# Layer 0's operator products and scan steps on VectorE, its squares on ScalarE and TensorE, and a last norm that takes token blocks one by one

## The chip, the cores and the metric

The kernel is one program on one core of a Trainium2 chip. The core's engines are TensorE (PE: matmuls; PEld: its weight loads), VectorE (DVE), ScalarE (ACT), GpSimd (POOL) and SyncE (SP), which issues most DMAs. Each engine takes its instructions in the order in which they stand in its own queue; an instruction whose inputs aren't ready holds up all behind it. The metric is the time of one execution on the device in microseconds. The kernel before takes 2677.52 us, the median of three runs (2677.16 to 2686.56).

## The reference

One step of a streaming encoder with two layers and width 1024, on 1024 prompt tokens and 8 running streams of 16 tokens (1152 columns in all). Layer 0 mixes an S5 state space model with a gated DeltaNet; layer 1 is sliding-window attention; each is followed by a SwiGLU. Cut to what the change touches:

```python
def rmsnorm(x, w):
    xf = x.astype(jnp.float32)
    y = xf * lax.rsqrt(jnp.mean(xf * xf, axis=-1, keepdims=True) + RMS_EPS)
    return (y * w.astype(jnp.float32)).astype(x.dtype)

def l2norm(x):
    return x * lax.rsqrt(jnp.sum(x * x, axis=-1, keepdims=True) + L2_EPS)

# S5, in chunks of 64 tokens
lam_bar = jnp.exp(lam * dt)
b_bar = ((lam_bar - 1.0) / lam)[..., None] * lax.complex(b_re, b_im)
def step(carry, u_blk):
    bu = jnp.einsum('gpc,btgc->btgp', b_bar, u_blk.astype(jnp.complex64))
    bu = bu.at[:, 0].add(lam_bar * carry)
    _, xs = lax.associative_scan(combine, (a_blk, bu), axis=1)
    y_blk = jnp.einsum('gcp,btgp->btgc', c, xs).real
    return xs[:, -1], y_blk

# DeltaNet: causal conv of width 4 and silu on q, k, v; q and k through l2norm;
# 4 heads of 128 in chunks of 64 with a triangular solve, then a recurrence over chunks
```

## The kernel before, in words

Activations lie with features on partitions: x is four tiles of 128 partitions by 2 feature chunks by 1152 tokens, so there are 8 chunks of features (k) and 3 blocks of 384 tokens (b). An fp32 product is made of three matmuls of split operands (whi, wlo, as in L320 to L322 and L459 to L461); the feed-forward products use a scheme with fewer products, whose panels B11, T1, B21, B22, T2, T3, T4 are summed into x by L836 and L888 as they come out of the banks.

Layer 0 runs in this order. Norm 0 (the loop over b from L987): ScalarE squares the 8 chunks of a block, POOL adds them in pairs (L1000), and `rms` (L366 and on) sums the four pairs over partitions by fp32 matmuls with a matrix of ones (L376). Meanwhile `s5_coefs` builds the S5 operators: a chain of small POOL and ScalarE steps makes lambda's powers (c tiles, L1676 to L1754), then for each of four parts m VectorE and POOL multiply the powers by B and C (L1777 to L1800, `every` at L1750). Their results lb and cl go out by DMA and come back as matmul operands, first for the states XE (pe, L1084). TensorE meanwhile projects the input; its bank evictions ut (L976) and zz (L1042) are VectorE's.

Then comes the scan over chunks: 15 dependent steps, each with two multiplications by the powers L (L1099) and two adds (L1100, L1101), all on POOL; 8 small steps that carry the state FE between groups of 16 chunks (L1105 to L1107), and 7 times two products of 128x512 on POOL (L1111), added to XE by VectorE (L1112, L1113). Beside it run the four DeltaNet heads: projections come out of banks into cr (L1134 to L1137, VectorE), the convolution is four VectorE steps (L1144, L1146), silu makes cy (ScalarE and VectorE, L1152, L1169), the squares of q and k are POOL's (L1164), summed by matmuls (L333), and the head's products A and AQ are finished by VectorE (L1201 to L1209). After the last head come a triangular solve, transfers and the recurrence, then the output product and layer 0's feed-forward.

The scheduler of the framework orders each engine's queue from its own model of times and from priorities that the code gives (`Sooner`). So the order is a result of the whole program, and it changes when an instruction changes its engine.

The last norm is a closure `final` (L1628 to L1648) that the last feed-forward calls through `fill` as chunks of x get final. It squares and adds chunks as they come (`square_in`), calls `rms` for a block, and then scales: chunks 0, 3 and 6 by ScalarE and POOL (L1641, L1642), the other five by VectorE (L1644); an output DMA takes two chunks (L1646). In the code, `final` is set up when panel T2 is done, for all three blocks (L897 and on).

## Time and profile before

| | |
|---|---|
| median of 3 runs | 2677.52 us |
| the profiled execution | 2678.2 us |
| its span in the trace | 2676.4 us |
| TensorE (PE) busy | 2524.3 us, 94% |
| VectorE (DVE) busy | 1986.1 us, 74% |
| POOL busy | 1624.0 us, 61% |
| ScalarE (ACT) busy | 1187.3 us, 44% |

The time of the profiled execution includes 1.8 us around the span. A share over the whole span is a mean over stretches that are bounded by different engines; the stretches that the change touches are the first 430 us and the last 30, and the rows below are taken from these. A busy time of an engine in the trace is from an instruction's start to its end, whatever held it up inside.

### The profile page before, as it was taken

What the parts mean: (1) busy time and instruction counts of PE and PEld (TensorE: products, weight loads), DVE (VectorE), ACT (ScalarE), POOL (GpSimd) and SP (SyncE); (2) the same over time, 40 slices, a digit from 0 to 9 for tenths busy, and PEclk for the clock granted to TensorE, in tenths of its full rate; (3) what the DMA queues carried; (4) which work ended last, traced back from release to release, by engine and by line L of the source; (5) the groups of instructions that cost most, each with busy time, mean ns of one, the idle gap of its engine ahead of it and who ended that gap; (6) DMA issues with size and microseconds to landing.
All of it is one profiled execution on the core that took longest, in us unless ns stands there. A gap on an engine that the chain in (4) does not pass through costs nothing.

```text
span 2676.4 us, 40734 instructions
## 1 busy us (share of the span) xinstructions
PE 2524.3 (94%) x14897; PEld 2403.3 (90%) x14897; DVE 1986.1 (74%) x3255; ACT 1187.3 (44%) x2411; POOL 1624.0 (61%) x1659
## 2 busy tenths in 40 slices
PE   7898899999899999989999999999899999989996
PEld 5787798998799999989998988788789999989996
DVE  7847874567877877788867245667878777788967
ACT  5234466344634444444334145655644444444333
POOL 8739532125598888878633012214598888878735
PEclk9899999999999999989999999999999999989998
DMA  6432377643132222244212200203122222243211
GB/s 211 122 121 72 109 230 225 190 130 118 37 106 76 75 76 87 84 158 134 84 50 103 74 25 25 96 31 103 40 96 89 75 77 75 86 167 127 90 50 71
DMA packets 164167, 267.23 MB, mean 100 GB/s; under 512 B 34188, under 2 KB 123948, under 8 KB 162928
## 3 DMA queue, kind: packets, MB, share of 16 engines
q1 hardware_dynamic: 163392, 262.28, 30.4%
q8 instruction: 117, 1.92, 0.3%
q10 hardware_dynamic: 576, 2.36, 0.2%
q14 instruction: 82, 0.67, 0.1%
HBM read 186.92 MB, written 79.51 MB: 100 GB/s over the span
## 4 chain that ended last, share of the span: by engine, by line
PE 69%; POOL 11%; DVE 10%; DMA 4%; issue 4%; ACT 2%; SPq 0%; DVEq 0%; POOLq 0%; ACTq 0%
PE pa L461 7%; PE pa L459 7%; PE pa L460 7%; PE pd L459 4%; PE pd L460 4%; PE pd L461 4%; PE pg L320 3%; PE b L459 3%; PE pg L322 3%; PE pg L321 3%; PE b L460 3%; PE b L461 3%; PE pg L1549 2%; PE pg L1550 2%; PE pg L1551 2%
## 5 line engine op out<-in xcount | busy, mean ns | idle before, releaser
L459 PE MATMUL pa<-u,whi 128*128 128x384 f32 x904 | 307.2, 341 | 20.0 <-ACT whi L541 10.3
L460 PE MATMUL pa<-u,whi 128*128 128x384 f32 x904 | 306.1, 339 | 1.1 <-DVE u L269 1.1
L461 PE MATMUL pa<-u,wlo 128*128 128x384 f32 x904 | 298.8, 339 | 7.7 <-DVE wlo L542 7.7
L541 ACT CAST whi<-x 128x1024 fp32r<-128x1024 f32 (+2 forms) x184 | 132.2, 745 | 256.9 <-PE pa L460 164.6
L460 PE MATMUL pd<-g,whi 128*128 128x384 f32 x708 | 241.2, 341 | 0.0
L459 PE MATMUL pd<-g,whi 128*128 128x384 f32 x708 | 240.1, 339 | 0.0
L461 PE MATMUL pd<-g,wlo 128*128 128x384 f32 x708 | 238.2, 338 | 0.0
L542 DVE TENSOR_TENSOR wlo<-x,whi 128x1024 fp32r<-128x1024 f32 (+2 forms) x184 | 210.4, 1165 | 24.4 <-ACT whi L541 24.3
L1907 POOL TENSOR_SCALAR p<-p,rd 128x192 f32<-128x192 f32 (+3 forms) x80 | 59.1, 741 | 249.6 <-DVE rd L1901 132.9
L459 PEld LDWEIGHTS pa<-u,whi 128*128 128x128 f32 x904 | 171.5, 190 | 24.9 <-ACT whi L541 13.9
L297 ACT CAST whi<-raw 128x1024 fp32r<-128x1024 f32 x113 | 116.8, 1048 | 172.5 <-PE pg L321 76.0
L537 POOL TENSOR_TENSOR x<-x 128x256 f32<-128x256 f32 (+1 forms) x186 | 171.2, 942 | 25.5 <-DVE wlo L542 18.7
L298 DVE TENSOR_TENSOR wlo<-raw,whi 128x1024 fp32r<-128x1024 f32 x113 | 164.7, 1460 | 21.6 <-ACT whi L297 20.4
L537 POOL TENSOR_TENSOR x<-raw 128x256 f32<-128x256 f32 (+1 forms) x186 | 169.2, 931 | 18.9 <-DVE wlo L542 11.0
L461 PEld LDWEIGHTS pa<-u,wlo 128*128 128x128 f32 x904 | 171.5, 190 | 9.2 <-DVE wlo L542 9.0
L537 POOL TENSOR_TENSOR cm<-raw 128x256 f32<-128x256 f32 (+1 forms) x150 | 145.1, 990 | 47.3 <-DVE wlo L542 18.9
L460 PEld LDWEIGHTS pa<-u,whi 128*128 128x128 f32 x904 | 171.7, 190 | 2.1 <-DVE u L269 1.7
L459 PE MATMUL pa<-u,x 128*128 128x384 f32 x428 | 146.6, 343 | 5.3 <-ACT x L541 2.8
L320 PE MATMUL pg<-h0h,whi 128*128 128x384 f32 x384 | 136.1, 354 | 12.3 <-DVE ut L976 11.4
L460 PE MATMUL pa<-u,x 128*128 128x384 f32 x428 | 145.6, 340 | 0.0
L461 PE MATMUL pa<-u,x 128*128 128x384 f32 x428 | 142.4, 341 | 0.0
L796 DVE TENSOR_TENSOR g<-gf,g 128x384 fp32r<-128x384 f32 x132 | 136.4, 1060 | 5.4 <-ACT g L795 5.4
(744 smaller groups left out, 8223.5 us busy)
## 6 DMA issues: line engine op xcount, KB each, us to landing
gf<-d_g SPq DMA_DIRECT2D x44, 576.0 KB
raw<-in_wd_dram SPq DMA_DIRECT2D x44, 512.0 KB
raw<-in_wg_dram SPq DMA_DIRECT2D x24, 512.0 KB
raw<-in_wu_dram SPq DMA_DIRECT2D x24, 512.0 KB
raw<-in_win_dram SPq DMA_DIRECT2D x21, 512.0 KB
x<-in_wg_dram SPq DMA_DIRECT2D x20, 512.0 KB
x<-in_wu_dram SPq DMA_DIRECT2D x20, 512.0 KB
d_r<-x SPq DMA_DIRECT2D x24, 384.0 KB
```

Of the source, the lines that this page charges most:

```text
L297: S.copy(hi, raw)
L298: V.tensor_sub(lo, raw, hi)
L320: PE.matmul(p[:, :BW], hi[:, c], rh, start=(i == 0), stop=False)
L321: PE.matmul(p[:, :BW], hi[:, c], rl, start=False, stop=False)
L322: PE.matmul(p[:, :BW], lo[:, c], rh, start=False, stop=(i == len(ks) - 1))
L459: PE.matmul(p, hi[:, c], uh, start=start, stop=False, skip_group_check=more)
L460: PE.matmul(p, hi[:, c], ul, start=False, stop=False, skip_group_check=more)
L461: PE.matmul(p, lo[:, c], uh, start=False, stop=stop, skip_group_check=more)
L537: (P.tensor_add if sg > 0 else P.tensor_sub)(cm[:, 256 * j:256 * (j + n)], fa, ga)
L541: S.copy(hi[:, c], src)
L542: V.tensor_sub(lo[:, c], src, hi[:, c])
L796: eng.tensor_sub(op[1], t, op[0])
```

## The change

Four parts lie in layer 0's mixer. In norm 0 POOL's twelve adds are gone and the matmuls with ones sum all 8 squares of a block (24 in place of 12). In `s5_coefs` the products t2, t3, tl and tc (16 instructions) are VectorE's. In the scan, all of POOL's 60 step instructions, the 24 small ones and the 14 of 128x512 are VectorE's. The 24 squares of `l2norms` are ScalarE activations. The fifth part replaces `final` by a class `Final`: block 0 is squared, normed and sent out as soon as its panels are final, before the last panels of the other blocks; the partition sums take more parts by matmul (2, 3 and 6 for the three blocks, where it was 3 each); the scale is left in the PSUM bank p and read from there by the products (L1696 of the new file); ScalarE and POOL take chunks 0 to 2 of block 0 and 0 and 1 of block 1, and none of block 2; the table of logarithms is loaded once, at block 0.

```diff
--- before.py
+++ after.py
@@ -890,12 +890,26 @@
                                 fill(x, 4 + m, 1, 4 + m)
                             if n == "B22":
                                 fill(x, m, 2, 4 + m)
+                                if m == 3 and not nxt:
+                                    fin.out(x, 1)
+                                    fin.out(x, 2)
                     if q < 2 and e == 0:
                         for m in range(4):
                             into([(W[i], 512 * i2, G[i][f"f{i2}"]) for i in range(2) for i2 in range(2)] + plain(4 * q + m, 0), m, x[:, 4 * q + m, blk(0)])
+                    if last and not nxt and q == 1 and e == 0:
+
+                        t = [hp.tile([128, 4, BW], F32, name="sq", tag="h", bufs=4 * NB) for _ in range(4)]
+                        fin = Final([a[:, i] for a in t for i in range(4)])
+                        fill = fin.fill
+                        for k in range(KC):
+                            fill(x, k, 0, k)
+                        fin.out(x, 0)
+                        for k in range(4):
+                            fill(x, k, 1, k)
                     if last and n == "T2":
                         for m in range(4):
                             into(plain(4 + m, 2), m, x[:, 4 + m, blk(2)])
+                    if last and nxt and n == "T2":
                         room = itertools.cycle([s12[0][:, :BW], s12[0][:, BW:2 * BW], s12[1][:, :BW]])
                         fill = nxt(lambda: next(room), s12[1][:, BW:2 * BW], rr)
                         for k in range(KC):
@@ -996,9 +1010,7 @@
                 V.tensor_scalar(h[b][k][0], x[:, k, blk(b)], wk, None, op0=ALU.mult)
             V.scalar_tensor_tensor(h[b][k][1], x[:, k, blk(b)], wk, h[b][k][0], ALU.mult, ALU.subtract)
             S.activation(q[k], x[:, k, blk(b)], AF.Square)
-            if k % 2:
-                P.tensor_add(q[k], q[k], q[k - 1])
-        ln += rms(r, b, q[1::2])
+        ln += rms(r, b, q)
         for w, ev in zip(W, (ev_ba, ev_uu)):
             tag = next(room)
             gemm_block(w, h, b, ev, p=tag and mbank(tag))
@@ -1096,19 +1108,19 @@
     for c in range(1, 16):
         t = sc[:, 0:16].rearrange("p (a k) q g -> p a k q g", k=2)
         for k in range(2):
-            P.tensor_tensor(t[:, :, k], L8[:, k][:, None].to_broadcast([128, 8, 2, 16]), XG[:, :, c - 1], ALU.mult)
-        P.tensor_tensor(XG[:, :, c], XG[:, :, c], t[:, :, 0], ALU.add)
-        P.tensor_tensor(XG[:, :, c], XG[:, :, c], t[:, :, 1, ::-1, :], ALU.add)
+            V.tensor_tensor(t[:, :, k], L8[:, k][:, None].to_broadcast([128, 8, 2, 16]), XG[:, :, c - 1], ALU.mult)
+        V.tensor_tensor(XG[:, :, c], XG[:, :, c], t[:, :, 0], ALU.add)
+        V.tensor_tensor(XG[:, :, c], XG[:, :, c], t[:, :, 1, ::-1, :], ALU.add)
     P.memset(FE[:, 0], 0.0)
     for a in range(8):
         t = sc[:, 0:2]
-        P.tensor_tensor(t, PW[:, :, 15], FE[:, a][:, None].to_broadcast([128, 2, 2, 16]), ALU.mult)
-        P.tensor_tensor(FE[:, a + 1], XG[:, a, 15], t[:, 0], ALU.add)
-        P.tensor_tensor(FE[:, a + 1], FE[:, a + 1], t[:, 1, ::-1, :], ALU.add)
+        V.tensor_tensor(t, PW[:, :, 15], FE[:, a][:, None].to_broadcast([128, 2, 2, 16]), ALU.mult)
+        V.tensor_tensor(FE[:, a + 1], XG[:, a, 15], t[:, 0], ALU.add)
+        V.tensor_tensor(FE[:, a + 1], FE[:, a + 1], t[:, 1, ::-1, :], ALU.add)
     for a in range(1, 8):
         t = sc[:, 2:34].rearrange("p (k c) q g -> p k c q g", k=2)
         for k in range(2):
-            P.tensor_tensor(t[:, k], PW[:, k], FE[:, a][:, None].to_broadcast([128, 16, 2, 16]), ALU.mult)
+            V.tensor_tensor(t[:, k], PW[:, k], FE[:, a][:, None].to_broadcast([128, 16, 2, 16]), ALU.mult)
         V.tensor_tensor(XG[:, a], XG[:, a], t[:, 0], ALU.add)
         V.tensor_tensor(XG[:, a], XG[:, a], t[:, 1, :, ::-1, :], ALU.add)
     Q.dma_start(O["s5p"], XE[:, TP // CS - 1])
@@ -1161,7 +1173,7 @@
             for b in range(NB):
                 s = blk(b)
                 sq = cv.tile([128, BW], F32, name="sq", tag="sq", bufs=2)
-                P.tensor_mul(sq, y[:, s], y[:, s])
+                S.activation(sq, y[:, s], AF.Square)
                 act.append(behind(S.activation(rr[:, s], sums(sq, BW), AF.Ln, bias=epsc), tables))
         for y, rr, f in ys:
             act.append(S.activation(rr[:, :T], rr[:, :T], AF.Exp, scale=-0.5, bias=f))
@@ -1625,29 +1637,66 @@
     x, c_x, pre = swa(locals())
 
 
-    def final(new, keep, r):
-        ...
+    class Final:
+        PARTS = {0: (7,), 1: (6, 7), 2: (3, 4, 5, 6, 7)}
+        GP = {0: (0, 1, 2), 1: (0, 1), 2: ()}
+
+        def __init__(self, rooms):
+            it = iter(rooms)
+            self.r = [[next(it) for _ in range(3)] for b in range(NB)]
+            rest = list(it)
+            self.late, self.new = {0: [self.r[0][2]], 1: [self.r[1][2], self.r[2][2]], 2: rest[:5]}, itertools.cycle(rest[5:])
+            self.parts = [[], [], []]
+
+        def fill(self, x, k, b, i):
+            s, parts = blk(b), self.parts[b]
+            if i == 0:
+                q = self.r[b][0]
+            elif i not in self.PARTS[b]:
+                q = next(self.new)
+            else:
+                q = self.late[b][i - self.PARTS[b][0]]
+            S.activation(q, x[:, k, s], AF.Square)
+            if i and i not in self.PARTS[b]:
+                P.tensor_add(parts[0], parts[0], q)
+            else:
+                parts.append(q)
+            if k in self.GP[b]:
+                S.activation(x[:, k, s], x[:, k, s], AF.Copy, scale=nw[:, 4 * KC + k:4 * KC + k + 1])
+            if i == KC - 1:
+                self.rms(b)
+
+        def rms(self, b):
+            p = mbank("pn", "pd" if b == 2 else "pn")[:, :BW]
+            parts = self.parts[b]
+            for i, sq in enumerate(parts):
+                PE.matmul(p, onesf, sq, start=(i == 0), stop=(i == len(parts) - 1))
+            y, v = self.r[b][0], self.r[b][1]
+            tables = [] if b else [tc.keep_in_program_order(log_tables())]
+            behind(S.activation(y, p, AF.Ln, scale=1.0 / D, bias=epsc), *tables)
+            V.tensor_scalar(v, p, 1.0 / D, EPS, op0=ALU.mult, op1=ALU.add)
+            S.activation(y, y, AF.Exp, scale=-0.5)
+            V.scalar_tensor_tensor(v, y, -0.5, v, ALU.mult, ALU.mult)
+            V.tensor_mul(v, v, y)
+            V.scalar_tensor_tensor(p, v, 1.5, y, ALU.add, ALU.mult)
+            if self.GP[b]:
+                S.copy(y, p)
+            self.scale = {**getattr(self, "scale", {}), b: (p, y)}
+
+        def out(self, x, b):
             s = blk(b)
+            p, y = self.scale[b]
+            for i, t in enumerate(x.tiles):
+                for k in (2 * i, 2 * i + 1):
+                    if k in self.GP[b]:
+                        P.tensor_mul(x[:, k, s], x[:, k, s], y)
                     else:
+                        V.scalar_tensor_tensor(x[:, k, s], x[:, k, s], nw[:, 4 * KC + k:4 * KC + k + 1], p, ALU.mult, ALU.mult)
+                Q.dma_start(O["y"][2 * i:2 * i + 2, :, s].rearrange("k p t -> p k t"), t[:, :, s])
+
-    ffn(x, pre, 1, 3, final)
+    ffn(x, pre, 1, 3, None)
     c_x()
     for c in (M["close"], c_pg, c_dr, c_rp, c_hp, c_wp, c_cons):
         c()
@@ -1775,17 +1824,17 @@
         B, C = (t[:, :, m].rearrange("p k (g c) -> p k g c", c=16) for t in (Ball, Call))
         B1 = B1p
         V.tensor_mul(B1, g16(fr[:, gs]), B[:, 0])
-        P.tensor_mul(t2, g16(fi[:, gs]), B[:, 1])
+        V.tensor_mul(t2, g16(fi[:, gs]), B[:, 1])
         V.tensor_add(B1, B1, t2)
         V.tensor_mul(B2, g16(fr[:, gs]), B[:, 1])
-        P.tensor_mul(t3, g16(fi[:, gs]), B[:, 0])
+        V.tensor_mul(t3, g16(fi[:, gs]), B[:, 0])
         V.tensor_sub(B2, B2, t3)
 
         V.tensor_scalar(C[:, 0], C[:, 0], sgn, -1.0, op0=ALU.mult, op1=ALU.mult)
         V.tensor_scalar(C[:, 1], C[:, 1], -1.0, None, op0=ALU.mult)
         lb, tl = (cf.tile([128, 8, CS, 16], F32, name=n, tag=n, bufs=1) for n in ("lb", "tl"))
         every(V, lb, PR[:, CS - 1::-1, gs], B1)
-        every(P, tl, PIs[:, ::-1, gs], B2)
+        every(V, tl, PIs[:, ::-1, gs], B2)
         V.tensor_add(lb, lb, tl)
         lt = cf.tile([128, 8, 128], F32, name="lt", tag="lt", bufs=1)
         for g0 in (0, 4):
@@ -1796,7 +1845,7 @@
         Q.dma_start(d_lb[m].rearrange("p (g i) -> p g i", g=8), lt)
         cl, tl = (cf.tile([128, 8, CS + 1, 16], F32, name=n, tag=n, bufs=1) for n in ("cl", "tc"))
         every(V, cl, PR[:, :, gs], C[:, 0])
-        every(P, tl, PI[:, :, gs], C[:, 1])
+        every(V, tl, PI[:, :, gs], C[:, 1])
         V.tensor_add(cl, cl, tl)
         Q.dma_start(d_cl[m].rearrange("p (g i) -> p g i", g=8), cl[:, :, 1:, :].rearrange("p g e c -> p g (e c)"))
         kt = cf.tile([16, 8, 128], F32, name="kt", tag="kt", bufs=1)
```

On VectorE, the operators before (lb, cl: products of powers with B and C; tc: POOL's partner; ut: evictions of the projection; L298: the low part of a split weight):

```order
L1750 TENSOR_TENSOR lb<-c_582,B1p 128x1024
L1750 TENSOR_TENSOR cl<-c_582,C 128x1152
L976 TENSOR_TENSOR ut<-pg,r 128x48x8
L1021 TENSOR_SCALAR XE<-XE 4x1152
L976 TENSOR_TENSOR ut<-pg,r 128x48x8
L1800 TENSOR_TENSOR cl<-cl,tc 128x1152
L1022 SCALAR_TENSOR_TENSOR RT<-XE 4x1152
L1026 TENSOR_TENSOR XE<-RT 4x1024
```

and now, with `every` at L1799:

```order
L1799 TENSOR_TENSOR lb<-c_582,B1p 128x1024
L1799 TENSOR_TENSOR cl<-c_582,C 128x1152
L298 TENSOR_TENSOR wlo<-raw,whi 128x1024
L1799 TENSOR_TENSOR tc<-c_583,C 128x1152
L1031 SCALAR_TENSOR_TENSOR XE<-XE 4x1152
L990 TENSOR_TENSOR ut<-pg,r 128x48x8
L1799 TENSOR_TENSOR tl<-c_627,B_1044 128x1024
L1849 TENSOR_TENSOR cl<-cl,tc 128x1152
L1033 TENSOR_SCALAR XE<-XE 4x1152
L990 TENSOR_TENSOR ut<-pg,r 128x48x8
L1838 TENSOR_TENSOR lb<-lb,tl 128x1024
```

The partners tc and tl (POOL's before) stand between the evictions ut and the old products, and each VectorE sum has both of its factors in the same queue.

On VectorE, at the start of the scan and the first head, before (cst: the running streams' states; cr: evictions of projections; ca: the convolution; Dm: a head's decay matrix):

```order
L1146 SCALAR_TENSOR_TENSOR ca<-cr,cw,ca 128x1176
L1092 TENSOR_TENSOR XE<-XE,cst 128x8x32
L1134 TENSOR_TENSOR cr<-pg,r 128x384
L1146 SCALAR_TENSOR_TENSOR ca<-cr,cw,ca 128x1176
L1197 SCALAR_TENSOR_TENSOR Dm<-pB,CN,mask 128x128 x3
L1146 SCALAR_TENSOR_TENSOR ca<-cr,cw,ca 128x1176
L1134 TENSOR_TENSOR cr<-pg,r 128x384
L1206 COPY GL<-AQ 128x3
```

and now (L1111 to L1113 are the scan steps, L_98 the powers, ssq the product):

```order
L1111 TENSOR_TENSOR ssq<-L_98,XE 128x8x32 x2
L1209 SCALAR_TENSOR_TENSOR Dm<-pB,CN,mask 128x128 x3
L1112 TENSOR_TENSOR XE<-XE,ssq 128x8x32
L1148 TENSOR_TENSOR cr<-pg,r 128x256
L1149 TENSOR_TENSOR cr<-pg,r 128x8x16
L1113 TENSOR_TENSOR XE<-XE,ssq 128x8x32
L1111 TENSOR_TENSOR ssq<-L_98,XE 128x8x32 x2
L1112 TENSOR_TENSOR XE<-XE,ssq 128x8x32
L298 TENSOR_TENSOR wlo<-raw,whi 128x1024
L1113 TENSOR_TENSOR XE<-XE,ssq 128x8x32
L1146 TENSOR_TENSOR cr<-pg,r 128x384
```

The scan steps that were POOL's stand between evictions, splits and head products. With the scan's steps in VectorE's queue, an eviction cr behind them waits for them.

On VectorE, in the tail, before (x_18814, x_18818, x_22837 and x_22839 are the four tiles of x, pn the bank of a sum):

```order
L836 TENSOR_TENSOR x_18818<-x_18818,pd 128x384
L1644 SCALAR_TENSOR_TENSOR x_18814<-x_18814,nw,r 128x384
L1644 SCALAR_TENSOR_TENSOR x_18818<-x_18818,nw,r 128x384
L1644 SCALAR_TENSOR_TENSOR x_22837<-x_22837,nw,r 128x384 x2
L1644 SCALAR_TENSOR_TENSOR x_22839<-x_22839,nw,r 128x384
L836 TENSOR_TENSOR x_18818<-x_18818,pd 128x384
L379 TENSOR_SCALAR ssq<-pn 128x384
L364 TENSOR_TENSOR s_24764<-s_24764 128x384
L381 SCALAR_TENSOR_TENSOR nt<-r,ssq 128x384
L364 TENSOR_TENSOR s_24764<-s_24764,s_24763 128x384
```

and now (L1679 to L1683 make a block's scale, L1696 scales a chunk):

```order
L836 TENSOR_TENSOR x_18818<-x_18818,pd 128x384 x2
L1679 TENSOR_SCALAR sq<-pn 128x384
L1681 SCALAR_TENSOR_TENSOR sq<-sq 128x384
L1682 TENSOR_TENSOR sq<-sq 128x384
L1683 SCALAR_TENSOR_TENSOR pn<-sq 128x384
L1696 SCALAR_TENSOR_TENSOR x_18818<-x_18818,nw,pn 128x384 x2
L1696 SCALAR_TENSOR_TENSOR x_22837<-x_22837,nw,pn 128x384 x2
L1696 SCALAR_TENSOR_TENSOR x_22839<-x_22839,nw,pn 128x384 x2
L1679 TENSOR_SCALAR sq<-pn 128x384
L1681 SCALAR_TENSOR_TENSOR sq<-sq 128x384
L1682 TENSOR_TENSOR sq<-sq 128x384
L1683 SCALAR_TENSOR_TENSOR pn<-sq 128x384
```

The last of the evictions stood behind the products of block 1; now both stand ahead of its norm and products, and block 0 no longer appears here. The order of all engines is the same between layer 0's feed-forward and the last panels.

## Rows read from the trace of the kernel before

**Rows 1.** The page's first line.

```profile
span 2676.4 us, 40734 instructions
```

**Rows 2.** Busy times of stretches: stretch, length, busy us (instructions) by engine, clock, DMA.

```profile
core 0: us, PE busy (x) PEld busy (x) DVE busy (x) ACT busy (x) POOL busy (x), PEclk, DMA share, GB/s
45.00:125.00 80.00, 57.26 (x312) 51.14 (x311) 62.55 (x53) 24.71 (x40) 69.19 (x109) 0.87 0.41 112
63.90:124.00 60.10, 44.35 (x239) 39.50 (x239) 54.90 (x44) 15.06 (x29) 51.70 (x55) 0.85 0.40 105
125.00:176.00 51.00, 51.00 (x363) 47.11 (x362) 14.29 (x18) 16.43 (x25) 1.52 (x9) 1.00 0.53 171
176.40:354.80 178.40, 160.14 (x876) 142.66 (x875) 146.04 (x236) 80.67 (x161) 132.43 (x158) 0.97 0.28 89
320.00:430.00 110.00, 102.23 (x647) 97.94 (x647) 70.78 (x145) 72.90 (x110) 32.57 (x78) 0.97 0.66 206
430.00:2600.00 2170.00, 2096.98 (x12467) 2016.45 (x12466) 1626.24 (x2713) 964.12 (x2028) 1324.55 (x1225) 0.99 0.28 92
```

**Rows 3.** The chain of waits, 40 to 430 us: start us, us, what.

```profile
174.39 0.68 PE pe L1084 x8
...
176.38 1.84 POOL ssq L1099 x2
...
325.52 0.65 PE pn L333 x2
```

**Rows 4.** Groups on POOL, 0 to 130 us: count, busy us, mean ns, idle before.

```profile
L1000 POOL TENSOR_TENSOR sq<-sq,sq 128x384 f32<-128x384 f32 x12 | 14.5, 1212 | 4.9 <-ACT sq L998 4.8
L1750 POOL TENSOR_TENSOR tc<-c,C 128x1152 f32<-128x1152 f32 x4 | 10.0, 2500 | 0.1
L1750 POOL TENSOR_TENSOR tl<-c,B 128x1024 f32<-128x1024 f32 x4 | 8.2, 2053 | 2.5 <-DVE lb L1789 2.4
```

**Rows 5.** Groups on POOL, 176.4 to 354.8 us.

```profile
L1099 POOL TENSOR_TENSOR ssq<-L,XE 128x256 f32<-128x256 f32 x30 | 28.8, 979 | 9.5 <-ACT XE L1085 9.0
L1164 POOL TENSOR_TENSOR sq<-cy 128x384 f32<-128x384 f32 x24 | 22.5, 944 | 15.9 <-ACT cy L1152 10.7 <-PE pn L333 5.2
```

**Rows 6.** Single lines on VectorE: duration in ns minimum/median/maximum, starts, forms.

```profile
L1750 DVE TENSOR_TENSOR lb<-c,B1p x4: 1225/1532/1925, 63.9 to 117.7; 128x1024 f32<-128x1024 f32 x4
L1750 DVE TENSOR_TENSOR cl<-c,C x4: 1347/2296/3205, 65.0 to 119.6; 128x1152 f32<-128x1152 f32 x4
...
L1091 DVE TENSOR_TENSOR cst<-x0e,L x2: 418/629/840, 144.1 to 176.8; 128x256 f32<-128x256 f32 x2
...
L1112 DVE TENSOR_TENSOR XE<-XE,ssq x7: 693/1257/1762, 258.5 to 296.1; 128x512 f32<-128x512 f32 x7
...
L1146 DVE SCALAR_TENSOR_TENSOR ca<-cr,cw,ca x36: 1427/1440/2460, 162.7 to 394.3; 128x1176 f32<-128x1176 f32 x36
...
L1169 DVE TENSOR_TENSOR cy<-cy,ca x24: 544/581/1178, 201.1 to 341.9; 128x384 f32<-128x384 f32 x24
```

**Rows 7.** Groups on VectorE, 176.4 to 354.8 us.

```profile
L1146 DVE SCALAR_TENSOR_TENSOR ca<-cr,cw,ca 128x1176 f32<-128x1176 f32 x27 | 43.7, 1619 | 0.3
L1169 DVE TENSOR_TENSOR cy<-cy,ca 128x384 f32<-128x384 f32 x24 | 17.4, 776 | 1.8 <-ACT ca L1167 1.8
```

**Rows 8.** Waits of TensorE, 176.4 to 354.8 us: total, times, longest.

```profile
PE pn L333 <- POOL sq L1164: 10.3, 5, 5.8
```

**Rows 9.** Timeline of the tail: start us, us, engine line op, idle before.

```profile
2650.76 0.55 DVE L836 TENSOR_TENSOR x<-x,pd 128x384 f32<-128x384 f32 x1
...
2660.09 5.04 DVE L1644 SCALAR_TENSOR_TENSOR x<-x,nw,r 128x384 f32<-128x384 f32 x5
...
2667.49 4.94 DVE L1644 SCALAR_TENSOR_TENSOR x<-x,nw,r 128x384 f32<-128x384 f32 x5
```

**Rows 10.** Single lines, ns minimum/median/maximum: VectorE with a PSUM operand, ScalarE's squares.

```profile
L497 DVE SCALAR_TENSOR_TENSOR x<-x,nw,pn x48: 601/608/615, 640.9 to 1901.1; 128x384 f32<-128x384 f32 x48
...
L360 ACT ACTIVATE s<-x x42: 507/522/529, 1393.9 to 2658.1; 128x384 f32<-128x384 f32 x42
```

More of the change, by code (lines that the diff above doesn't have):

```diff
@@ L1625, in body @@
     x, c_x, pre = swa(locals())
-    def final(new, keep, r):
-        parts = []
-        def fill(x, k, b, i):
-            s = blk(b)
-            square_in(x, k, b, i, new, parts, keep)
-            if i < KC - 1:
-                return
-            rms(r, b, parts)
-            with Sooner(0 if b == NB - 1 else -300):
-                for i in range(KC):
-                    wk = nw[:, 4 * KC + i:4 * KC + i + 1]
-                    if i in (0, 3, 6):
-                        S.activation(x[:, i, s], x[:, i, s], AF.Copy, scale=wk)
-                        P.tensor_mul(x[:, i, s], x[:, i, s], r[:, s])
-                    else:
-                        V.scalar_tensor_tensor(x[:, i, s], x[:, i, s], wk, r[:, s], ALU.mult, ALU.mult)
-                for i, t in enumerate(x.tiles):
-                    Q.dma_start(O["y"][2 * i:2 * i + 2, :, s].rearrange("k p t -> p k t"), t[:, :, s])
-        return fill
```

## The prediction

> **What bounds the kernel now.** I read the page first, then the busy times of stretches, then the chain of waits. From 430 to 2600 us TensorE is busy 2096.98 of 2170 us [rows 2]: there nothing is to be had, and the order of that work is the same before and after, so a stretch that starts earlier ends earlier by as much. The change lies in the stretches outside it. From 45 to 125 us TensorE is busy 57.26 of 80 us, while POOL has 69.19 and VectorE 62.55 [rows 2]: it waits for the S5 operators. From 125 to 176 it is busy all 51.00 us [rows 2]. At 176.38 the chain goes over from the matmuls to the scan on POOL [rows 3], and from 176.4 to 354.8 (the last product of the last head's matrix) POOL is busy 132.43 us, VectorE 146.04, TensorE 160.14 of 178.4 [rows 2]. No engine is full over this stretch, but the chain runs along POOL's in-order queue, and TensorE waits there for POOL's squares, 10.3 us in five pieces [rows 8]. At the end VectorE alone works through three norms after the last matmuls [rows 9].
>
> **Norm 0.** Twelve POOL adds go, 14.5 us [rows 4]. TensorE gets twelve more fp32 matmuls with the ones matrix at 0.65 us (the two on record make one: the chain shows 0.65 for x2 [rows 3]), 7.8 us, less the POOL adds that it no longer waits for. I cost TensorE's part at zero: it lies ahead of a stretch in which TensorE idles 22.7 of 80 us for another reason [rows 2]. Without that cover it would be up to 7.8. What counts is that POOL's chain for lambda, its powers and the factors is queued behind these adds. That chain is also bound to ScalarE's sines, which stay behind the norm's own activations, so the start of the operators (63.9) can move by anything from nothing to 14.5 us. I take 8: a little over half, since the adds are spread and only the late ones stand directly in front.
>
> **Operators on VectorE.** They run from 63.9 to 124.0 with VectorE busy 54.90 and POOL 51.70 of 60.10 us [rows 2]. The four tc products took 10.0 us and the four tl 8.2 on POOL [rows 4]; with the eight small ones, which I put at 7 from their share of columns and the same stretching, some 25 us leave. On VectorE the twins of the same shape show their undisturbed minimum: 1.35 us for cl, 1.23 for lb [rows 6], so 4 x 1.35 + 4 x 1.23 + 8 x 0.3 = 12.7 us are added. Against that, VectorE's own products are stretched now: cl has minimum 1.35 and median 2.30 [rows 6], and some of the others stretch alike. If all of that stays, VectorE needs 54.9 + 12.7 = 68 us, 8 longer than the stretch; if it goes, about 54.9 - 12 + 12.7 = 56 us, 4 shorter. I take the second, since POOL keeps only the small power products and stops before them. So the scan starts 8 + 4 = 12 us earlier, with bounds of 0 and 18; TensorE's 51 full us from 125 to 176 pass this on one to one.
>
> **Scan and heads.** Added to VectorE: 30 multiplications of 128x256 by a broadcast, which POOL did in 979 ns [rows 5] and VectorE's twin does in 0.418 us undisturbed [rows 6], 12.5 us; 30 adds of the same size, 12.5 us; 14 of 128x512 at 0.69 us (the minimum of the add of that shape [rows 6]), 9.7 us; 24 tiny ones at an estimated 0.2, 5 us. Sum 40 us. Taken off VectorE: what the neighbour on POOL costs it. L1146 has a mean of 1619 ns in this stretch and a minimum of 1427, x27 makes 5.2 us; L1169 776 and 544, x24, 5.6 us [rows 6, 7]; the other two-input groups, by the same reading, I put at 11 more. So 146 + 40 - 22 = 164 us of VectorE work. That is more than TensorE's 160.14 and less than today's 178.4: VectorE becomes the engine that bounds this stretch, and it has to be nearly full. I take 165, a gain of 13. With no relief it is 146 + 40 = 186, a loss of 8; the other end is TensorE's 160, a gain of 18. The scan steps are queued on VectorE between evictions of projection banks and head products, so each eviction behind them comes later by one or two steps, up to about a microsecond; that is already in the sum of a full queue. The 24 squares go to ScalarE at 0.52 us [rows 10] instead of 944 ns on POOL [rows 5], 12.5 us on an engine that is busy 80.67 of 178.4 [rows 2]; the 10.3 us of TensorE's waits for them vanish, but they lie inside the same stretch and are no second gain.
>
> The Trainium skill (SBUF — State Buffer, Terms) says VectorE and GpSimd share one port pair as an exclusive lock, held for a whole instruction. By that rule the whole stretching of VectorE's two-input products would vanish with the POOL products, as the minima beside the medians suggest; taken strictly, the two engines could not have been busy 54.90 and 51.70 of 60.10 us at once, unless busy time contains blocked time, which the trace does not separate.
>
> The Trainium skill (VectorE: DVE Perf Modes, Rules for kernel authors) advises to keep the count of chained VectorE instructions low, since each one drains. That speaks against 24 tiny steps in the scan's chain; at 0.4 us each, twice my price, the stretch would lose 5 us more. No row of before shows one of them on VectorE.
>
> **Behind the heads.** The solve, its transfers and the recurrence follow the last head product. From 320 to 430 TensorE is busy 102.23 of 110 us and the DMA share is 0.66 [rows 2]; about 14 us of panel matmuls will now stand behind the last head product, as VectorE and not TensorE sets the pace ahead of it. Of the 25 us gained up to there I let 4 go here (bounds 0 and 8). Mixer: 12 + 13 - 4 = 21 us.
>
> **Last norm.** Before: the eviction at 2650.76 is followed by five products of block 1, the last norm's five begin at 2667.49 and take 4.94, their POOL neighbours running beside; VectorE ends at 2672.43 and the last transfer 4.0 us later, at the span's end [rows 1, 9]. After, block 0 is out long before, so the walk is: both last evictions to 2651.8; the square 0.52 and the two activations of block 1, 1.1, to 2653.5; three VectorE steps of 0.6 to 2655.3; six products with the scale read from a bank at 0.61, the price of a like instruction with a PSUM operand [rows 10], to 2659.0; block 2's four steps, 2.3, to 2661.3; eight products, 4.9, to 2666.2; the transfer, 4.0, to 2670.2. That is 6 us (bounds 3 and 9: 3 if each product costs the 1.0 us of the five at 2660.09 [rows 9], because ScalarE and POOL still work beside them). The extra matmuls, 11 for 9, hide behind the same evictions, all but the last at 0.65.
>
> **Sum.** 2678.2 us of the profiled execution - 21 - 6 = 2651; the median of the runs is 0.7 below that execution, so 2650.5.
>
> **The rivals.**
> 1. VectorE takes over as bound without much relief (chance 0.14). The stretch to 354.8 stays at about 178, and only the earlier start, less the 4 us behind the heads, and the tail are left: 2677.5 - 8 - 6 = 2664. For it: VectorE already shows 146.04 of 178.4. Against it: the minima of [rows 6], which only occur when POOL is quiet.
> 2. The gain is swallowed ahead of the recurrence (0.13): transfers and the solve's fixed chain bound 355 to 430, and half of the 25 us goes. 2677.5 - 12 - 6 = 2659. For it: the DMA share 0.66 there; against it: most of these transfers are issued when a head is done and move with it.
> 3. Slower (0.06): the stretching of VectorE's products does not come from POOL. Then the operators take 68 us in place of 60, which eats the 8 us of the earlier start, and the heads' VectorE work is 186 us, which at a queue that is 93% full (146 + 40 over 200) takes 200 instead of 178.4. 2677.5 + 22 - 6 = 2693. It decides for slower as soon as the heads' stretch is longer than about 184 us, with the start unchanged.
> 4. The squares come no earlier from ScalarE than from POOL, because its queue holds a wait for a bank in front of them (0.04): the 10.3 us of waits stay and TensorE, not VectorE, paces the heads at 170: some 5 us worse than forecast, 2655.
>
> **Chances.** The forecast has 0.63, with a range of its own of 2637 to 2663. A measurement can tell 0.5%, 13.4 us, from no change. Faster by more than that (under 2664): 0.63 + 0.13 + 0.04 + a little of rival 1, 0.81. Within it: most of rival 1, 0.13. Slower: 0.06. The range of 2632 to 2671 leaves out rival 3 and the best ends of all terms together (18 + 18 - 0 + 9 = 45 us gained).
>
> **What would show it.** After: lb's first operator product should start near 56 in place of 63.9, with cl at 1.35 to 1.6 us throughout; the first scan multiplication near 164 on VectorE at 0.42 to 0.5 us; the head stretch about 165 us long with VectorE over 90% busy and POOL nearly idle; no wait of TensorE for squares over a microsecond; the start of layer 0's FFN some 21 us earlier; then equal pace up to the last norm, and the last VectorE product some 4 to 6 us after block 2's scale. The forecast is wrong if VectorE's mean for L1146 stays at 1.6 us, if the head stretch is over 175, or if the FFN starts less than 10 us earlier.

## The result and the profile after

The changed kernel takes 2646.44 us, the median of four runs (2634.92 to 2649.54), where the kernel before takes 2677.34; the ratio is 0.9868 (95% interval 0.985 to 0.9885), some 31 us to the good. A second set of five runs gave 2645.14 and 0.9874 (0.9856 to 0.9892). The forecast was 2650.5 with a range of 2632 to 2671: right in sign and size. Several of its terms were off and made up for each other.

The page of the kernel after begins so (compare [rows 1]; the second line has busy time and share of each engine):

```profile
span 2643.3 us, 40745 instructions
...
PE 2527.9 (96%) x14925; PEld 2409.6 (91%) x14925; DVE 1971.5 (75%) x3367; ACT 1199.6 (45%) x2435; POOL 1476.2 (56%) x1509
```

VectorE got 112 more instructions and is busy 14.6 us less. That is the first sign that what it lost was no work but stretching. The stretches that answer to [rows 2], with the same columns, are 59.7 to 119.1 for the operators, from the first product lb to the end of their last sum (63.9 to 124.0 before), 115 to 167 for the states, and 168.6 to 328.4 for scan and heads (176.4 to 354.8 before). The line from 60 to 80 shows the operators' first third by itself:

```profile
45.00:115.00 70.00, 60.28 (x341) 56.74 (x340) 59.40 (x79) 25.61 (x40) 42.85 (x72) 0.93 0.48 129
115.00:167.00 52.00, 52.00 (x369) 47.51 (x369) 19.14 (x26) 16.58 (x26) 1.93 (x11) 1.00 0.53 179
59.70:119.10 59.40, 53.70 (x319) 50.18 (x317) 55.15 (x61) 18.55 (x32) 29.59 (x34) 0.94 0.50 134
60.00:80.00 20.00, 18.81 (x115) 17.82 (x115) 19.81 (x19) 7.89 (x8) 19.40 (x22) 1.00 0.28 80
168.60:328.40 159.80, 153.01 (x851) 140.19 (x850) 147.19 (x329) 87.89 (x181) 16.24 (x32) 0.97 0.30 95
430.00:2600.00 2170.00, 2102.19 (x12402) 2019.52 (x12402) 1620.13 (x2708) 961.47 (x2024) 1331.81 (x1226) 0.98 0.27 88
```

Scan and heads take 159.8 us in place of 178.4. VectorE is busy 147.19 us there, with 93 instructions more for 1.2 us more; POOL fell from 132.43 to 16.24. TensorE is now the fullest, 153.01 of 159.80.

The same single lines as in [rows 6], now in the kernel after (minimum/median/maximum in ns):

```profile
L1799 DVE TENSOR_TENSOR cl<-c,C x4: 1347/1366/1873, 60.9 to 112.3; 128x1152 f32<-128x1152 f32 x4
L1799 DVE TENSOR_TENSOR tc<-c,C x4: 1348/1368/1591, 63.3 to 107.5; 128x1152 f32<-128x1152 f32 x4
...
L1111 DVE TENSOR_TENSOR ssq<-L,XE x30: 411/421/439, 168.6 to 226.8; 128x256 f32<-128x256 f32 x30
...
L1158 DVE SCALAR_TENSOR_TENSOR ca<-cr,cw,ca x36: 1427/1440/1457, 148.8 to 373.0; 128x1176 f32<-128x1176 f32 x36
...
L1181 DVE TENSOR_TENSOR cy<-cy,ca x24: 549/555/562, 196.8 to 317.0; 128x384 f32<-128x384 f32 x24
```

The reader should look at the maxima. The minima are within 1% of those of [rows 6]. In the heads the maxima (2460 for the convolution and 1178 for cy before) have come down to within 3% of the minima: there the minimum of before was the undisturbed price. Among the operators this holds for the medians, but not for every single product: the cl of 1873 ns runs at 79 us, while POOL still makes powers and is busy 19.40 of 20 us.

Where the 33.1 us of the two spans went, by events that both traces have:

| event | before | after | earlier by |
|---|---|---|---|
| first operator product lb | 63.9 | 59.7 | 4.2 |
| last eviction ut of the projection begins | 129.5 | 116.1 | 13.4 |
| last state matmul pe | 175.3 | 167.2 | 8.1 |
| first scan product | 176.4 | 168.6 | 7.8 |
| last head product A ends | 354.8 | 328.4 | 26.4 |
| solve begins | 366.6 | 344.8 | 21.8 |
| layer 0's feed-forward begins | 668.1 | 647.5 | 20.6 |
| layer 1's output product begins | 1668.0 | 1639.4 | 28.6 |
| layer 1's output product ends | 1883.9 | 1861.5 | 22.4 |
| last panel matmul begins | 2650.0 | 2624.8 | 25.1 |
| end of the span | 2676.4 | 2643.3 | 33.1 |

The lead also moves where the change touches nothing. It grows by 8.0 us between the start of layer 0's feed-forward and layer 1's output product, and 6.2 us of it go again along that product. Layer 1 is not ordered alike in the two kernels: along its output product VectorE has the same instructions in another order, for example reductions `ng<-pS` and evictions `o1l<-pO` change places. The statement ahead of the prediction that the order is the same from layer 0's feed-forward to the last panels does not hold there. Why that product takes 222 us in one kernel and 216 in the other was not found. Its first and last matmuls, before and after:

```profile
L1549 PE MATMUL pg<-o0h,whi x72: 334/336/448, 1668.0 to 1792.0; 128*128 128x384 f32 x72
L1549 PE MATMUL pg<-o0h,wf x24: 338/338/636, 1858.8 to 1883.9; 128*128 128x384 f32 x24
```
```profile
L1561 PE MATMUL pg<-o0h,whi x72: 331/336/668, 1639.4 to 1756.6; 128*128 128x384 f32 x72
L1561 PE MATMUL pg<-o0h,wf x24: 338/338/636, 1836.4 to 1861.5; 128*128 128x384 f32 x24
```

The tail before has one thing that [rows 9] do not show. The eviction at 2650.76 is the last but one; the last stands behind a group of five products. Three such groups follow each other (2651.22, 2660.09, 2667.49), one for each block, so the first is block 0's and not block 1's:

```profile
2649.95 0.34 PE L461 MATMUL pd<-g,wlo 128*128 128x384 f32 x1
...
2651.22 5.43 DVE L1644 SCALAR_TENSOR_TENSOR x<-x,nw,r 128x384 f32<-128x384 f32 x5
...
2656.58 0.54 DVE L836 TENSOR_TENSOR x<-x,pd 128x384 f32<-128x384 f32 x1
```

The tail of the kernel after (timeline):

```profile
2624.84 0.34 PE L461 MATMUL pd<-g,wlo 128*128 128x384 f32 x1
...
2625.29 0.55 DVE L836 TENSOR_TENSOR x<-x,pd 128x384 f32<-128x384 f32 x1 [2.28 <-PE pd L461]
...
2629.93 3.24 DVE L1696 SCALAR_TENSOR_TENSOR x<-x,nw,pn 128x384 f32<-128x384 f32 x6 [0.60 <-ACT sq L1685]
2629.97 1.95 POOL L1694 TENSOR_TENSOR x<-x,sq 128x384 f32<-128x384 f32 x2 [4.96 <-ACT sq L1685]
...
2635.53 4.29 DVE L1696 SCALAR_TENSOR_TENSOR x<-x,nw,pn 128x384 f32<-128x384 f32 x8
```

Eight products take 4.29 us where five took 5.04. The six of block 1 follow each other at 0.54 us; POOL's two products run beside the first 1.95 of their 3.24 us. From the start of the last panel matmul to the span's end it is 18.5 us; it was 26.4.

### The profile page after: what moved, and what is told of

It is laid out like the page before. It is cut to its first block, busy times and chain, and to the rows that moved or that the text cites. A ratio compares the mean times of both kernels' runs of the same rounds, so it can differ in the third digit from the quotient of the medians.

```text
span 2643.3 us, 40745 instructions
## 1 busy us (share of the span) xinstructions
PE 2527.9 (96%) x14925; PEld 2409.6 (91%) x14925; DVE 1971.5 (75%) x3367; ACT 1199.6 (45%) x2435; POOL 1476.2 (56%) x1509
## 4 chain that ended last, share of the span: by engine, by line
PE 70%; DVE 9%; POOL 5%; ACT 3%; issue 2%; DMA 2%; SPq 0%; DVEq 0%; POOLq 0%; ACTq 0%
PE pa L459 7%; PE pa L461 7%; PE pa L460 7%; PE pd L461 4%; PE pd L459 4%; PE pd L460 4%; PE b L459 4%; PE b L461 4%; PE b L460 4%; PE pg L320 3%; PE pg L321 3%; PE pg L322 3%; PE pg L1561 2%; PE pg L1562 2%; PE pg L1563 2%
## 5 line engine op out<-in xcount | busy, mean ns | idle before, releaser
L459 PE MATMUL pa<-u,whi 128*128 128x384 f32 x904 | 307.6, 341 | 18.6 <-DVE bt L574 10.0
L297 ACT CAST whi<-raw 128x1024 fp32r<-128x1024 f32 x113 | 116.9, 1050 | 175.3 <-PE pg L321 80.7
L537 POOL TENSOR_TENSOR x<-raw 128x256 f32<-128x256 f32 (+1 forms) x186 | 169.7, 934 | 18.6 <-DVE wlo L542 10.9
L298 DVE TENSOR_TENSOR wlo<-raw,whi 128x1024 fp32r<-128x1024 f32 x113 | 162.7, 1441 | 18.9 <-ACT whi L297 18.7
```

The costliest lines, as they stand in the source:

```text
L297: S.copy(hi, raw)
L298: V.tensor_sub(lo, raw, hi)
L459: PE.matmul(p, hi[:, c], uh, start=start, stop=False, skip_group_check=more)
L537: (P.tensor_add if sg > 0 else P.tensor_sub)(cm[:, 256 * j:256 * (j + n)], fa, ga)
```

## The experiments

My theory: POOL's two-input products and VectorE's stretch each other, and POOL's queue with the scan set the pace of the heads. Rivals: TensorE's waits for squares were the cost; the operators' start was; or VectorE's durations have nothing to do with POOL. Five kernels undo one part of the change each, two add one part to the kernel before, two add work on POOL that nobody reads, one undoes two parts, and two repeat. When one instruction changes its engine, the scheduler gives all queues of the mixer a new order, so a difference of some us between two kernels holds the new order too. That is so in layer 1 as well, far behind the mixer. There the output product takes from 212 to 223 us from kernel to kernel, and two executions of the changed kernel, whose order is the same, have 222.1 and 222.7. So besides the total the texts below give how far a kernel is ahead or behind when that product begins, at 1639.4 us in the changed kernel.

**The scan back on POOL**

```diff
-            V.tensor_tensor(t[:, :, k], L8[:, k][:, None]..., XG[:, :, c - 1], ALU.mult)
+            P.tensor_tensor(t[:, :, k], L8[:, k][:, None]..., XG[:, :, c - 1], ALU.mult)
...
```

> The change with one part undone: the scan's 60 steps, the 24 small ones and the 14 products of 128x512 are on POOL again, all else as in the changed kernel. My theory: the scan on POOL and VectorE's two-input products stretch each other and POOL's queue sets the pace of the head stretch, so this part carries most of the gain: 12 to 20 us more than the changed kernel (2658 to 2666), with VectorE's convolution step (128x1176) back to a mean near 1.6 us in the head stretch and that stretch near 178 us. Rival (TensorE's waits for squares are what cost): squares are still ScalarE's, so the stretch stays near 165 us and the time within 5 us of the changed kernel.

Measured 2659.24 us, ratio 0.9934 (0.9922 to 0.9946): 13 us more than the changed kernel. The first scan product starts at 168.0 and the last head product ends at 346.4, 178.4 us, to the tenth what it was before. VectorE's group there, then POOL's (count, busy us, mean ns):

```profile
L1158 DVE SCALAR_TENSOR_TENSOR ca<-cr,cw,ca 128x1176 f32<-128x1176 f32 x25 | 39.9, 1595 | 0.1
```
```profile
L1111 POOL TENSOR_TENSOR ssq<-L,XE 128x256 f32<-128x256 f32 x30 | 30.5, 1040 | 4.2 <-ACT XE L1097 3.2
```

The convolution step is back at 1595 ns, and TensorE has no squares to wait for from POOL. The rival of the squares falls. When layer 1's output product begins, this kernel is 20.1 us behind the changed one; 6.6 of these come back along that product. How much of the 18.6 us of the heads is stretching, and how much is the scan's own slower steps in POOL's queue (1040 ns where VectorE takes 422), these runs do not separate.

**The squares back on POOL**

```diff
-                S.activation(sq, y[:, s], AF.Square)
+                P.tensor_mul(sq, y[:, s], y[:, s])
```

> The change with one part undone: the 24 squares of q and k are on POOL again, all else as in the changed kernel. My theory: with the scan gone from POOL its queue is empty, the squares are ready when asked for, TensorE does not wait for them, and VectorE is stretched by at most 24 times some 0.4 us: 0 to 6 us more than the changed kernel. Rival (the waits for squares cost by themselves): 10 us more.

Measured 2638.83 us, ratio 0.9855 (0.9842 to 0.9867), which is neither: some 7 us *less* than the changed kernel. It was run again:

> The kernel with the squares alone back on POOL, once more, on a chip together with the others. Its ratio to the kernel before was 0.9855 (0.9842 to 0.9867), that of the changed kernel 0.9868 (0.985 to 0.9885) and 0.9874 (0.9856 to 0.9892). If the squares on POOL are really better, the ratio comes out below 0.9865 again; if the difference was the clock's, it may come out anywhere from 0.985 to 0.989.

Measured 2639.0 us, ratio 0.985 (0.9832 to 0.9868). The intervals overlap those of the changed kernel, but both medians, and 7 of 8 runs, lie below both of its medians. A ratio of 0.985 lies in both ranges that I had written down, so the repeat did not decide between them. In the first of the two VectorE is busy 153.8 us in the heads, some 7 more than in the changed kernel with as many instructions, and single scan products take up to 1050 ns, so the squares on POOL do stretch it. Even so the heads end at 327.4, 1.0 earlier than in the changed kernel; the solve begins at 341.2 (344.8; in the second trace at 341.7), and TensorE is busier behind it. The changed kernel, then this one, from 342 to 390 us:

```profile
342.00:390.00 48.00, 42.20 (x271) 40.33 (x271) 36.02 (x80) 36.08 (x45) 21.19 (x53) 1.00 0.79 252
```
```profile
342.00:390.00 48.00, 45.76 (x307) 44.91 (x306) 35.63 (x77) 35.63 (x46) 20.92 (x54) 1.00 0.91 296
```

But this lead is gone again well before the end. When layer 1's output product begins, the two traces are 2.3 and 5.5 us *behind* the changed kernel, as my theory had it (0 to 6 more). The first of them is ahead only after that product, which it does in 212.6 us instead of 222.1; the second trace's span, 2643.9 us, is no shorter than the changed kernel's. The product's first and last matmuls in the first trace:

```profile
L1561 PE MATMUL pg<-o0h,whi x72: 331/336/522, 1641.7 to 1756.1; 128*128 128x384 f32 x72
L1561 PE MATMUL pg<-o0h,wf x24: 335/338/636, 1829.0 to 1854.3; 128*128 128x384 f32 x24
```

So nothing here shows that squares on ScalarE cost time. The one trace that is shorter gains in layer 1, which is ordered otherwise; what in that order does it is open.

**Squares alone on ScalarE, in the kernel before**

> The kernel before with one part alone: the 24 squares of q and k on ScalarE, the scan still on POOL. Theory 1 (the waits for squares behind the scan in POOL's queue cost, 10.3 us in the trace of before): 5 to 10 us faster, 2668 to 2673. Theory 2 (they lie inside a stretch that POOL's scan bounds anyway, but POOL has 22.5 us less to do there, so the scan ends sooner): up to 15 us faster. Theory 3 (ScalarE's queue delays head products, as the kernel with the squares put back on POOL seems to show, which was 7 us faster): the same or slower than before.

Measured 2673.86 us beside 2681.93, ratio 0.9969 (0.9956 to 0.9981). The waits of TensorE for squares are gone (0.4 us left of 10.3), yet the last head product starts at 357.0 (354.5 before) and the solve at 371.9 (366.6). The stretch did not get shorter. Layer 0's feed-forward begins at 673.0 (668.1) and layer 1's output product 2.2 us later than before; that product then takes 212.1 us instead of 215.9, and at its end this kernel is 1.6 us ahead, and 3.7 when the last panel matmul begins. So what its trace gains it gains from layer 1 on, not where the part is. Theory 2 falls; up to layer 1 it is theory 3, and theory 1 has only the total.

**The scan alone on VectorE, in the kernel before**

> The kernel before with one part alone: the scan (60 steps, 24 small ones, 14 products of 128x512) on VectorE, squares and operator products still on POOL. My theory (POOL and VectorE stretch each other; the squares on POOL come at once when the scan is gone from its queue): the head stretch falls from 178 to some 162 us and the time by 13 to 19 us, to 2659 to 2665. Rival (the scan needs the squares on ScalarE too, since the waits of TensorE for POOL's squares go on): less than 8 us of gain.

Measured 2665.87 us, ratio 0.9942 (0.993 to 0.9954), 16 us less than its neighbours of before. Scan and heads take from 176.7 to 338.2, 161.5 us, with the squares still on POOL; TensorE's waits for them fall to

```profile
PE pn L333 <- POOL sq L1164: 0.3, 1, 0.3
```

from the 10.3 of [rows 8]. The scan in front of them in POOL's queue was what made the squares late. VectorE is busy 160.32 of the 161.5 us.

**The operators back on POOL**

```diff
-        every(V, tl, PIs[:, ::-1, gs], B2)
+        every(P, tl, PIs[:, ::-1, gs], B2)
...
```

> The change with one part undone: the 16 operator products (t2, t3, tl, tc) are on POOL again, all else as in the changed kernel. My theory: the operators take about 60 us in place of some 55 and VectorE's products of 128x1152 go back to a median over 2 us: 3 to 8 us more than the changed kernel. Rival (VectorE's queue is the bound there, whatever POOL does, since it had 55 of 60 us busy before): taking 13 us off VectorE makes it the same or up to 5 us faster.

Measured 2654.18 us, ratio 0.992 (0.99 to 0.9941): 8 us more. The last ut begins at 127.4 (116.1), the last pe at 170.5 (167.2), the last A at 332.7 (328.0). When layer 1's output product begins, it is 8.1 us behind. On POOL the four tl take 11.4 us; on VectorE in the changed kernel their median is 1.24. My expectation for VectorE's products of 128x1152 missed: the median of cl stays at 1356 ns, and only one of them takes 3224. The rival, that VectorE's queue was the bound, falls.

**Norm 0's adds back on POOL**

```diff
-        ln += rms(r, b, q)
+            if k % 2:
+                P.tensor_add(q[k], q[k], q[k - 1])
+        ln += rms(r, b, q[1::2])
```

> The change with one part undone: POOL adds the squares of norm 0 in pairs again and TensorE sums four, all else as in the changed kernel. My theory: the adds stand ahead of POOL's chain for the powers, so the operators start 3 to 5 us later and the time grows by 3 to 6 us. Rival (TensorE's twelve matmuls less are worth more): the same time or up to 4 us faster.

Measured 2659.53 us, ratio 0.9933 (0.9917 to 0.9949): 13 us more, over twice what I expected. The trace explains part: the first lb 2.1 us later (I had said 3 to 5), the last pe 3.8, the last A 6.1, the solve 4.1. But layer 0's feed-forward begins 16.1 later, so 12 us arise between the solve and there. TensorE's clock falls in between; the stretches from 420 to 460 us show it at 0.72 and 0.77 of full, and the runs of this kernel had mean clocks of 0.969 to 0.977, where the changed kernel's first four had 0.980 to 0.988 and its second set 0.978 to 0.984:

```profile
420.00:440.00 20.00, 16.26 (x110) 14.46 (x109) 10.83 (x13) 9.75 (x16) 5.78 (x6) 0.72 0.97 317
440.00:460.00 20.00, 20.00 (x154) 18.86 (x152) 8.35 (x18) 5.96 (x12) 4.79 (x6) 0.77 0.21 68
```

TensorE idled 3.7 of 20 us at a DMA share of 0.97 just ahead of the recurrence. How much of the 13 us is the part's own, how much that pause's and how much layer 1's order (the span is only 9.6 us longer) is not settled.

**The last norm undone**

> The change with the last norm undone: the closure of the kernel before in place of the class, the mixer of the change. My theory: the parts are independent, since the work between them is the same and bounded by TensorE; the end comes 6 to 9 us later than in the changed kernel, 2652 to 2656, and the last block's products stand 7 to 8 us later behind the last matmul. Rival (the class only moves work from the tail into the stretch before it, where TensorE is busy): within 3 us of the changed kernel.

Measured 2653.22 us, ratio 0.9906 (0.9886 to 0.9925): 8 us more than the changed kernel on the same chip (2645.14); the two intervals just touch. Its last panel matmul begins at 2619.9 and its span ends at 2646.4, 26.5 us later, as before (26.4). So the part is worth the 8.0 us that the tails show, whatever the mixer does. The span is only 3.1 us longer than that of the changed kernel, since this execution was 3.6 us ahead when layer 1's output product began.

**The changed kernel again**

> The changed kernel once more, on the same chip as the others of this set, as the base that they are compared with. Its four runs spread from 2634.9 to 2649.5 us with granted clocks of 0.980 to 0.988. If the spread is the clock's, the runs here again order themselves by the clock, and the median lies at 2640 to 2650; if the first median was a chance value, it comes nearer to 2640, where the kernel with the squares on POOL was (2638.8).

Measured 2645.14 us (2641.10 to 2654.22). The first median was no chance value.

**Work on POOL that nobody reads**

```diff
+        for _ in range(4):
+            P.tensor_tensor(scr, XG[:, :, c], XG[:, :, c - 1], ALU.mult)      # x_pool2
+            P.tensor_scalar(scr, XG[:, :, c], 2.0, None, op0=ALU.mult)        # x_pool1 (in its place)
```

> The changed kernel with work added that nobody reads: after each of the 15 scan steps POOL makes four products of 128x256 from two SBUF inputs into a spare tile (60 in all, the count and size of the steps that were POOL's). VectorE does all that it does in the changed kernel. My theory (POOL's two-input products themselves stretch VectorE's two-input products): POOL's take 0.7 to 1 us each, VectorE's convolution step gets single values over 2 us and a mean of 1.5 to 1.6 us in the head stretch (1.44 in the changed kernel), the scan runs some 8 to 20 us longer than its 59 us, and the kernel gets 5 to 15 us slower. Rival (the stretching of before came from the queues, of VectorE waiting inside its instructions for POOL's results): VectorE's durations stay at 1.43 to 1.46 us and the time within 3 us.

> The changed kernel with work added that nobody reads: after each of the 15 scan steps POOL makes four scalings of 128x256 by a constant, one SBUF input each, into a spare tile (60 in all). If it is two-input work of POOL that stretches VectorE, this leaves VectorE's convolution step near 1.44 us or stretches it much less than the two-input twin does, and the time is within 5 us of the changed kernel. If any POOL work on SBUF does it, the two kernels look alike.

Measured 2689.86 us and 2694.58 us. VectorE's scan product L1112 (L1111 in the changed kernel, where its mean is 422 ns), beside two-input products and then beside one-input scalings, and then the convolution beside two-input products:

```profile
L1112 DVE TENSOR_TENSOR ssq<-L,XE 128x256 f32<-128x256 f32 x30 | 22.3, 780 | 0.3
...
L1161 DVE SCALAR_TENSOR_TENSOR ca<-cr,cw,ca 128x1176 f32<-128x1176 f32 x22 | 31.7, 1442 | 0.1
```
```profile
L1112 DVE TENSOR_TENSOR ssq<-L,XE 128x256 f32<-128x256 f32 x30 | 13.6, 491 | 0.3
```

The same instruction goes from 422 to 780 ns when POOL does two-input work that it does not depend on, and to 491 beside one-input work (the medians are 838 and 426 ns). That rules out waiting for POOL's results as the cause. My expectation for the convolution missed: in the new order it stands outside POOL's work and stays at 1442. The total times missed too, some 44 and 49 us more than the changed kernel where I had said 5 to 15 and at most 5: in both, the heads' products were ordered behind the scan, and TensorE waited for one bank's eviction:

```profile
PE pB L1199 <- ACT AQ L1213: 35.5, 2, 31.8
```

(43.0 us in the other.) These two kernels settle what POOL does to a duration, not what it does to the time.

**Squares and the small end of the scan on POOL**

> The changed kernel with two parts back on POOL: the 24 squares, and of the scan the 24 small steps and 14 products of 128x512; the 60 steps of the scan stay on VectorE. It asks whether VectorE, busy 160 of 170 us in the heads with the squares on POOL, is better off with less. My theory: what leaves VectorE (14.6 us) comes back as stretching (14 products of POOL at 1.3 us and more beside it), and TensorE is busy 97% there already: within 4 us of the kernel with the squares alone on POOL (2638.8). Rival (VectorE is what bounds): 5 to 10 us faster than that.

Measured 2657.19 us, ratio 0.9915 (0.9901 to 0.9929): 18 us more than with the squares alone there, both ways wrong. The 38 instructions took VectorE's adds of 128x512 from 0.69 to a mean of over 1 us (both wait for POOL's products of line L1123):

```profile
L1125 DVE TENSOR_TENSOR XE<-XE,ssq 128x512 f32<-128x512 f32 x7 | 8.6, 1224 | 2.5 <-POOL ssq L1123 2.5
L1124 DVE TENSOR_TENSOR XE<-XE,ssq 128x512 f32<-128x512 f32 x7 | 7.1, 1016 | 1.5 <-POOL ssq L1123 1.5
```

The last A comes at 335.8 (327.0). With 37 instructions fewer in the heads than with the squares alone on POOL, VectorE was busy no less (155.6 us and 153.8). The 8.8 us of the heads are half of the 18; where the rest arises was not found.

## Why the prediction was right, step by step

- **Start of the operators**: 8 us forecast, 4.2 measured. The kernel with the adds back on POOL loses 2.1 us here, the one with the operators back on POOL 1.0; what holds the rest is not shown.
- **Operators**: this step failed in size. 4 us shorter forecast, 60.1 to 59.4 measured. VectorE's busy time came out as said (55.15 us, forecast 56), so most of the stretching went. But POOL did not stop before these products: from 60 to 80 us it is busy 19.40 of 20 us, and single products are still stretched (1873 ns against 1347).
- **Passed on one to one by TensorE**: this step failed. 12 us forecast at the scan's start, 7.8 measured, though the last ut came 13.4 earlier. I had costed norm 0's extra matmuls at zero, under TensorE's idle time. The change itself used that cover up: from 45 to 115 TensorE is busy 60.28 of 70 us, and from 115 on it is full. Up to the last pe it idled 16.1 us less than before (32.6 before, 16.5 after) and was busy 8.0 us longer; the difference is the 8.1 us of the table. Of the 8.0, 6.4 are gone in the kernel with norm 0's adds back on POOL, so they belong to the extra matmuls for the most part.
- **Scan and heads**: 13 us forecast, 18.6 measured. The term that was mis-sized is the added work. The relief of 22 was about right: the durations of VectorE's old instructions, without the 98 new ones, cover 145.7 us of the stretch before and 118.8 after, 27 less, of which some 4 are five instructions that now stand outside the stretch. The 98 new ones last 39.9 us added up one by one, as forecast (the small steps 0.19 to 0.23 us each), but they make VectorE's busy time only 28.3 us longer, because an instruction begins before the one in front of it has ended. Two ssq of 0.42 us take 0.75 together; those of 128x512, 0.69 long, follow each other at 0.60:

```profile
183.37 0.75 DVE L1111 TENSOR_TENSOR ssq<-L,XE 128x256 f32<-128x256 f32 x2
```

  So VectorE has 147 us of work and not 164, and it was not the one bound of the stretch. TensorE is fuller, 153.01 of 159.80, but of the 6.8 us that it idles 6.5 fall into two slices in which VectorE is busy throughout (columns as in [rows 2]):

```profile
200.00:220.00 20.00, 18.92 (x120) 18.03 (x119) 20.00 (x42) 12.05 (x28) 2.42 (x4) 1.00 0.34 100
240.00:260.00 20.00, 14.54 (x72) 12.76 (x71) 20.00 (x43) 9.77 (x26) 0.68 (x3) 0.74 0.37 118
```

- **Squares**: no second gain was forecast, and none came. The waits vanish (no wait for squares in the stretch after), and the kernels with the squares on either engine end the heads within 1.0 us.
- **Behind the heads**: a loss of 4 forecast, 4.6 measured at the solve and 5.8 at the start of layer 0's feed-forward (20.6 us earlier, where I had said some 21). "Then equal pace" failed: the lead is 28.6 us at layer 1's output product, 22.4 at its end and 25.1 at the last panel matmul.
- **Last norm**: 6 forecast, 8.0 in the trace, 8 by the run that undoes it. The walk named the first five products as block 1's; they were block 0's. Its sum does not rest on that. Products with the scale in a bank follow each other at 0.54 us where it took 0.61.
- **Luck**: at the scan's start the forecast was 4 us too high, in the heads 6 us too low, so that the solve came 21.8 us earlier with 21 forecast for the mixer. That the sum fits so well is in part chance. The mechanism in the heads is not: with the scan back on POOL the convolution step and the stretch go back to what they were, and POOL work that nobody reads stretches VectorE's product from 422 to 780 ns.
- **Rivals**: 1 and 3 needed VectorE's durations to stay; in the heads they fell to their minima. 2 needed the gain to shrink by half ahead of the recurrence; 4.6 of 26.4 went. 4 did not happen: no wait for squares is left.

The Trainium skill (SBUF — State Buffer, Terms) has VectorE and GpSimd share one port pair under an exclusive lock. The added POOL work agrees in the main: 422 to 780 ns beside two-input products. It also shows 491 beside one-input ones, which is less than a full block; there the measurement decides.

## What to carry to other kernels

Before moving work between VectorE and POOL, compare minimum and maximum of VectorE's two-input instructions: where they are far apart only while POOL works, moving POOL's two-input work onto a VectorE that looks 80% busy can cost little, as here, where 98 more instructions left its busy time in the heads 1.2 us longer. Do not cost an edit at zero under idle time that the same change is about to remove. And judge each part by where in the trace it gains, not by its total alone: when the scheduler orders the whole program anew, a stretch that nobody edited can move by as much as the part. Here layer 1's output product moved by up to 10 us, and squares on ScalarE, which seemed to cost 7 us by the total, left the end of the heads within 1 us.

## What the runs showed of the hardware that was not expected

VectorE products whose scale lies in a PSUM bank follow each other at 0.54 us with POOL's two-input products beside the first of them, where the form with all operands in SBUF took 1.0 us [rows 9]. Short VectorE instructions overlap at their ends: two of 0.42 us take 0.75 together. And POOL's plain scaling of 128x256 has a median of 851 ns, more than its two-input product of that size (784), as far as the trace's spans on POOL can be trusted.
